# Two pairs of K tiles by seven products in the second half of an output projection too (one core, two-layer hybrid decoder trunk)

## The chip, the cores and the metric

The kernel runs on 1 core of one Trainium2 chip. The metric is the device time of one execution in microseconds (us). Three runs of the kernel before took 2124.72, 2124.95 and 2125.33 us; the median is 2124.95 us. A separate execution was recorded by the hardware profiler; its own time is 2124.64 us, of which the recorded span is 2122.9 us, so 1.74 us lie around the span.

Engine names as the profile has them: PE is the matrix engine, PEld its weight loads, DVE the vector engine, ACT the scalar engine, POOL the GpSimd engine, SP the engine that issues most DMAs (SPq is its queue).

## What is computed

Two layers, each with RMSNorm, a wide input projection, differential attention beside a gated short convolution, one shared output projection and a squared-ReLU MLP. Sequence 256, model width 2048, all in float32. The part that the change touches:

```python
for l in range(DEPTH):                                   # 2 layers
    h = _rmsnorm(x, attn_norm_g[l])
    proj = h @ w_in[l]
    ...
    conv = gate_b * _short_conv(gate_c * conv_in, conv_w[l])
    x = x + jnp.concatenate([attn, conv], axis=-1) @ w_out[l]    # 256x2048 @ 2048x2048
    hm = _rmsnorm(x, mlp_norm_g[l]) @ w_up[l]                    # 256x2048 @ 2048x8192
    x = x + jnp.square(jax.nn.relu(hm)) @ w_down[l]
```

## The kernel before

**Numbers.** A float32 operand is split into a high part (a copy in the type fp32r, made by ACT) and a low part (the operand minus the high part, made by DVE). A product is three matmuls (`TERMS`): high by high, high by low, low by high. A matmul of the output projection has 128 rows of K, 128 tokens as the stationary operand and 512 columns as the moving one.

**Output projection, first 1024 columns.** `BySeven.project` (line 823) computes column chunks 0 and 1 (512 columns each) side by side, in two accumulators of two PSUM banks. K has 16 tiles, taken as eight pairs. A plain pair costs 2 K tiles x 2 token tiles x 2 column chunks x 3 terms = 24 matmuls. Two of the pairs, 4 and 5 (the pairs whose activations are convolution outputs of `GATED`), go by seven products instead of eight (`seven`, line 851): seven products x 3 terms = 21 matmuls, in Winograd's form, with sums of the activations (`sums_of`) and sums of the weights (`BySeven.jobs`, line 777). Four products need accumulators of their own (three `bank` buffers and the `av` bank) until DVE has added them into x: e1 to e4, lines 885 to 901. The order is `self.order`: pairs 0 and 1 for chunk 0, then for chunk 1; seven with pair 4; pair 2; seven with pair 5; pair 3; pairs 6 and 7 for chunk 0 (after which chunk 0 and the e terms are added into x), then pairs 6 and 7 for chunk 1.

**Output projection, last 1024 columns.** The loop at line 984 does chunk 2 and then chunk 3 with `linear` (line 390): 16 K tiles x 2 token tiles x 3 terms = 96 matmuls each, then two additions into x.

**The weights' pipeline.** `Weights.take` hands out the next weight tile and issues the work for the ones up to three ahead (`AHEAD`). A plain job loads 512 KB (`raw`, 4 buffers) and splits it into `hi`/`lo` (`wpool`, 3 buffers). A job of a seven step loads two raws, splits the left one (`w7b`) and a quarter of the right one, and makes four sums (`w7t`) that are split as `w7x` and `w7y`. `w7b` and `w7t` come from `bpool` (8 buffers; four of them hold the projection's activations `cat` and one holds the activation sums `sf`), `w7x` and `w7y` from `apool` (4 buffers, which also hold the transposed parts below).

**From the projection to the MLP.** The MLP's norm is applied in pieces. `Norm.chunk(n)` takes chunk n of x: squares with row sums on ACT, eight transposes on PE into two `bank` buffers, and for each of four K tiles a high part on ACT and a low part on DVE (`split_gained`, line 285), both into tile `nT` n. `Norm.factors` sums the squares, makes the row factors on POOL, a diagonal matrix on DVE and, some ticks later, a matmul with it (`rbc`, line 531), which puts the ratio of the two token tiles' factors on all partitions. The first user of that ratio is the first `square` of the MLP.

**What sets the order.** PE runs in program order. A `Background` list holds pieces of work (generators), and `work.tick()`, called after every K tile of a projection (and after every four matmuls of the MLP's first part), advances them; `work.start(piece, wait)` and the numbers that a piece yields count ticks. DVE, ACT, POOL and SP are ordered by a planner that simulates the program; `late(ins)` keeps an instruction in program order instead. Chunks 0 and 1 are started after the first 1024 columns, with waits of 2 and 4 ticks and 2 more inside, so that their transposes run early in chunk 2's matmuls; chunk 2's run two K tiles into chunk 3's matmuls; chunk 3's run two ticks into the MLP.

**The MLP's start.** `up_part` (line 1147) works on a column of 128 units with half of K at a time: eight matmuls with 512 columns (high and low activations side by side), then eight with 256. The order is column 0 and column 1 with the first half of K (`nT` 0 and 1), then both with the second half (`nT` 2 for four K tiles, then `nT` 3). Every four matmuls tick once.

Of the kernel before, what the change touches and what calls it, by code (L numbers as in the profile page):

```python
# [9 lines left out]
F32 = mybir.dt.float32  # L10
F32R = mybir.dt.float32r
AF = mybir.ActivationFunctionType
ALU = mybir.AluOpType
# [20 lines left out]
NP = DFF // (2 * P)  # L34
LAG = 2
NB2 = DFF // (KG * P)


GATED = (0, 1)

# [82 lines left out]
def trunk(ctx: ExitStack, tc: tile.TileContext, x, w_in, w_out, conv_w, q_norm_g, k_norm_g,  # L123
# [22 lines left out]
    def wide(name):  # L146
        return nat.tile([P, CH], F32, tag="wide", name=name)
# [304 lines left out]
    class Norm:  # L452
# [57 lines left out]
            yield 1  # L510

        def factors(self):
            while self.squared < D // CH:
                yield 1
            tot = small.tile([P, NT], F32, tag="tot", name="tot", bufs=1)
            nc.vector.tensor_reduce(tot, self.ss, axis=AX.X, op=ALU.add)
            r = rstd_of(tot, D, "row", NT)
            self.r = small.tile([P, NT], F32, tag="rowf", name="rowf", bufs=2)
            nc.vector.tensor_copy(self.r, r)
            diag = wide("diag")[:, :NT * P].rearrange("p (t c) -> p t c", t=NT)  # L520
            if self.which:

                self.scale = small.tile([P, 1], F32, tag="rowf2", name="rowf2", bufs=1)
                nc.vector.tensor_mul(self.scale, r[:, 1:2], r[:, 1:2])
                ratio = small.tile([P, 1], F32, tag="ratio", name="ratio", bufs=1)
                nc.vector.reciprocal(ratio, r[:, 1:2])
                nc.vector.tensor_mul(ratio, ratio, r[:, 0:1])
                nc.vector.tensor_scalar_mul(diag[:, 0], ident, ratio)
                yield 8
                tp = bank("rbc")  # L530
                nc.tensor.matmul(tp[:, :P], ones, diag[:, 0], start=True, stop=True)
# [212 lines left out]
    class BySeven:  # L744
# [3 lines left out]
        def __init__(self, l, bpool, weights):  # L748
            self.l, self.pool, self.weights = l, bpool, weights
            n = D // (4 * P)  # L750
            seven = [n + q for q in GATED]
            plain = [i for i in range(2 * n) if i not in seven]


            self.order = [(n, i) for n in range(2) for i in plain[:2]]
            self.order += [step for i, j in zip(plain[2:], seven)
                           for step in (("seven", j), ("pair", i))]
            self.order += [("pair", i) for i in plain[2 + len(seven):-2]]
            self.order += [(n, i) for n in range(2) for i in plain[-2:]]
            self.sums = []  # L760

        def sums_of(self, q, y):
# [11 lines left out]
            nc.scalar.activation(hi, v, AF.Copy)  # L774
            nc.vector.tensor_sub(lo, v, hi.bitcast(F32))

        def jobs(self, w, i):

            mine = {}

            def split(hi, lo, src):
                nc.scalar.activation(hi, src, AF.Copy)
                nc.vector.tensor_sub(lo, src, hi.bitcast(F32))
                return hi, lo

            def two(pool, tag, name, src):

                room = pool.tile([P, 2, 2, CH], F32R, tag=tag, name=name)
                hi, lo = split(room[:, 0], room[:, 1], src)
                return [(hi[:, j], lo[:, j]) for j in range(2)]  # L790

            def plain():
                raws = []
                for n in range(2):
                    raw = self.weights.pool.tile([P, 2, CH], F32, tag="raw", name="raw", bufs=RAW)
                    nc.sync.dma_start(
                        raw, w[2 * P * i:2 * P * (i + 1), n * CH:(n + 1) * CH].rearrange(
                            "(k p) c -> p k c", p=P))
                    raws.append(raw)
                mine["raw"] = raws  # L800
                b11, b21 = two(self.pool, "b", "w7b", raws[0])
                hi = wpool.tile([P, 2, CH], F32R, tag="hi", name="whi")
                lo = wpool.tile([P, 2, CH], F32R, tag="lo", name="wlo")
                return b11, b21, split(hi[:, 0], lo[:, 0], raws[1][:, 1])

            def sums():
                left, right = mine["raw"]
                t = mine["t"] = self.pool.tile([P, 4, CH], F32, tag="b", name="w7t")

                nc.vector.tensor_sub(t[:, 0], right[:, 0], left[:, 0])  # L810
# [12 lines left out]
        def project(self, cat, norm, kpool, tmp):  # L823
            weights = self.weights
            both = [mm.tile([P, NT, CH], F32, tag="mm2", name=f"o{self.l}{n}") for n in range(2)]
# [43 lines left out]

            def onto(n):  # L870
                for t in range(NT):
                    nc.vector.tensor_add(xs[n][:, t], accs[n][t], xs[n][:, t])

            last = self.order[-1][1]
            steps = [i for what, i in self.order if what == "seven"]
            done = [j for j, (what, i) in enumerate(self.order) if what == 0][-1]
            for j, (what, i) in enumerate(self.order):
                if what == "pair":
                    plain(i, 0)
                    plain(i, 1)  # L880
                elif what == "seven":
                    seven(i, i == steps[0], i == steps[-1])
                    if i == steps[-1]:

                        x11, x21, x12, x22 = (xs[n][:, t] for n in range(2) for t in range(NT))


                        room = tmp.tile([P, 2, CH], F32, tag="ao", name="es", bufs=1)
                        e1, e2, e3 = room[:, 0], wide("e2"), room[:, 1]
                        e4 = kpool.tile([P, CH], F32, tag="kL", name="es4")  # L890
                        nc.scalar.activation(e1, prods[1], AF.Copy)
                        nc.vector.tensor_add(e2, prods[6], e1)
                        nc.vector.tensor_add(e4, prods[5], e2)
                        nc.vector.tensor_add(x22, prods[5], x22)
                        nc.vector.tensor_add(e3, prods[7], e2)
                else:
                    plain(i, what)
                    if j == done:
                        onto(0)
                        for x_, e in ((x11, e1), (x12, e4), (x21, e3), (x22, e3)):  # L900
                            nc.vector.tensor_add(x_, x_, e)
            onto(1)
            for n in range(2):
                work.start(norm.chunk(n, 2), 2 * n + 2)


    def mixer(l, norm, loads):

        with ExitStack() as scope:
# [18 lines left out]
            for what, i in by_seven.order:  # L928
                if what == "seven":
                    weights.jobs += by_seven.jobs(w_out[l], i)  # L930
                    continue
                for n in ((0, 1) if what == "pair" else (what,)):
                    weights.plain(w_out[l], 2 * P * i, n * CH, 2)
            for n in range(2, D // CH):
                weights.straight(w_out[l], 0, D // P, n * CH)
            loads(weights)

            bias = biasp.tile([P, 2 * NH, S], F32, tag="bias", name="bias")
# [45 lines left out]
            for n in range(2, D // CH):  # L984
                acc = linear(f"o{l}{n}", cat, weights)
                for t in range(NT):
                    nc.vector.tensor_add(xs[n][:, t], acc[:, t], xs[n][:, t])
                work.start(mnorm.chunk(n, 2))
        return mnorm

    def mlp(l, mnorm, last):
# [479 lines left out]
```

## Time and profile before

| what | us |
|---|---|
| runs, median (lowest to highest) | 2124.95 (2124.72 to 2125.33) |
| profiled execution, its own time | 2124.64 |
| its span | 2122.9 |
| busy: PE, DVE, ACT, POOL | 2117.9, 1724.9, 1376.8, 159.2 |
| layer 0: first 1024 columns of the output projection | 298.17 to 340.36 |
| layer 0: last 1024 columns | 340.36 to 386.71 |
| layer 1: last 1024 columns | 1395.63 to 1441.97 |

The page lists busy times over the span; matmuls are pipelined and a matmul's recorded duration overlaps the next one's, so the time that a matmul costs is read from the start of one stretch to the start of the next in the chain of waits, not from its recorded duration. In the chain of waits each row has a start, a length, the engine, the tile that is written, the line and a count. In a timeline each row has a start, a length, the engine, the line, the operation and what it writes and reads, a count, and in brackets how long the engine stood idle before it and for whom.

### The profile page before, as it was taken

The page shows a single profiled execution, that of the slowest core. Times are in us where ns is not written, and L with a number is a line of the kernel's source. Part 1 is how long each engine was busy: PE and PEld are TensorE (multiplying, and loading weights), DVE is VectorE, ACT ScalarE, POOL GpSimd, SP SyncE. Part 2 cuts the span into 40 slices and gives each one's busy share as a digit, 9 for nine tenths or more (in the row PEclk, how much of TensorE's full clock was granted, in tenths as well). Part 3 has the DMA queues.
Part 4 walks back from the last instruction along what each step waited for, and adds up shares of the span by engine and source line. Part 5 has one row for each costly group of instructions (what it writes and reads, how often), then busy time and mean ns, then how long its engine had stood idle before and what let it go on. Part 6 is the DMA issues. An engine that isn't in the chain of part 4 may idle for free.

```text
span 2122.9 us, 29237 instructions
## 1 busy us (share of the span) xinstructions
PE 2117.9 (100%) x10875; PEld 1812.2 (85%) x10875; DVE 1724.9 (81%) x2388; ACT 1376.8 (65%) x1828; POOL 159.2 (8%) x226
## 2 busy tenths in 40 slices
PE   9999999999999999999999999999999999999999
PEld 8888888888888888888888888888888888888887
DVE  6777677798888888799766776767988888888997
ACT  6777555677776776666566765556677677675664
POOL 3010100000000000011101101000000000000110
PEclk9999999999999999999999999999999999999999
DMA  8556657687777777788656565666877777777993
GB/s 274 177 166 192 195 189 233 213 252 225 231 233 232 235 231 230 253 299 289 217 170 183 164 207 180 199 208 222 259 233 232 232 229 233 233 229 259 319 309 104
DMA packets 297743, 476.01 MB, mean 224 GB/s; under 512 B 12707, under 2 KB 193781, under 8 KB 297600
## 3 DMA queue, kind: packets, MB, share of 16 engines
q1 hardware_dynamic: 269120, 406.76, 60.9%
q0 software_dynamic: 28288, 67.24, 10.0%
q8 instruction: 85, 1.39, 0.3%
q14 instruction: 58, 0.48, 0.1%
q10 hardware_dynamic: 192, 0.15, 0.0%
HBM read 440.52 MB, written 33.58 MB: 223 GB/s over the span
## 4 chain that ended last, share of the span: by engine, by line
PE 100%; DVE 0%; DVEq 0%; issue 0%
PE upc L1158 31%; PE pr L1201 14%; PE dn L1282 8%; PE ci L427 4%; PE gc L427 4%; PE gb L427 4%; PE q L403 4%; PE k L403 4%; PE v L403 4%; PE o L403 4%; PE o L838 3%; PE dn L1364 2%; PE dn L1201 2%; PE pr1r L1201 2%; PE pr0r L1201 1%; PE up L1158 1%
## 5 line engine op out<-in xcount | busy, mean ns | idle before, releaser
L320 DVE TENSOR_TENSOR wlo<-raw,whi 128x1024 fp32r<-128x1024 f32 x266 | 322.3, 1223 | 186.7 <-ACT whi L319 116.6
L1158 PE MATMUL upc<-nT,uhi 128*128 128x512 f32 x1920 | 454.7, 389 | 0.0
L319 ACT ACTIVATE whi<-raw 128x1024 fp32r<-128x1024 f32 x266 | 281.5, 1059 | 240.1 <-issue 29.0
L1158 PEld LDWEIGHTS upc<-nT,uhi 128*128 128x128 f32 x1920 | 360.2, 188 | 74.7
L1022 DVE TENSOR_TENSOR ulo<-uraw,uhi 128x1024 fp32r<-128x1024 f32 x256 | 312.1, 1223 | 118.9 <-ACT f L1190 89.3
L1021 ACT ACTIVATE uhi<-uraw 128x1024 fp32r<-128x1024 f32 x256 | 270.6, 1057 | 159.7 <-PE upc L1158 138.1
L1158 PEld LDWEIGHTS upc<-nT,ulo 128*128 128x128 f32 x1920 | 246.2, 191 | 9.4
L1158 PE MATMUL upc<-nT,ulo 128*128 128x256 f32 x1920 | 249.1, 283 | 0.0
L1282 PE MATMUL dn<-whi,fb 128*128 128x512 f32 x496 | 156.5, 389 | 0.0
L1047 ACT ACTIVATE b2h<-draw 128x1024 fp32r<-128x1024 f32 x83 | 88.1, 1061 | 48.5 <-PE pr L1201 41.3
L319 ACT ACTIVATE whi<-uraw 128x1024 fp32r<-128x1024 f32 x62 | 65.9, 1063 | 81.8 <-PE dn L1282 64.4
L1282 PEld LDWEIGHTS dn<-whi,fb 128*128 128x128 f32 x496 | 93.1, 188 | 19.3
L1168 ACT ACTIVATE ev<-upc 128x512 f32<-128x512 f32 x120 | 72.0, 600 | 53.8 <-PE upc L1158 53.8
L1047 ACT ACTIVATE t24h<-t 128x1024 fp32r<-128x1024 f32 x83 | 88.3, 1063 | 22.9 <-PE pr L1201 15.9
L1048 DVE TENSOR_TENSOR t24l<-t,t24h 128x1024 fp32r<-128x1024 f32 x83 | 101.4, 1221 | 1.7
L1048 DVE TENSOR_TENSOR b2l<-draw,b2h 128x1024 fp32r<-128x1024 f32 x83 | 101.4, 1221 | 1.1 <-ACT b2h L1047 1.1
L1048 DVE TENSOR_TENSOR t13l<-t,t13h 128x1024 fp32r<-128x1024 f32 x83 | 101.3, 1221 | 0.7
L1061 DVE TENSOR_TENSOR t<-draw 128x1024 f32<-128x1024 f32 x83 | 101.4, 1222 | 0.3
L1047 ACT ACTIVATE t13h<-t 128x1024 fp32r<-128x1024 f32 x83 | 88.3, 1064 | 13.3 <-DVE t L1061 2.9
L1282 PE MATMUL dn<-wlo,fb 128*128 128x512 f32 x248 | 96.5, 389 | 0.0
L1201 PE MATMUL pr<-t13h,f 128*128 128x512 f32 x240 | 93.8, 391 | 0.0
L320 DVE TENSOR_TENSOR wlo<-uraw,whi 128x1024 fp32r<-128x1024 f32 x62 | 75.9, 1224 | 17.9 <-ACT whi L319 17.5
(452 smaller groups left out, 4301.4 us busy)
## 6 DMA issues: line engine op xcount, KB each, us to landing
uraw<-in_w_up_dram SPq DMA_DIRECT2D x128, 1024.0 KB, 6.3
raw<-in_w_in_dram SPq DMA_DIRECT2D x191, 512.0 KB, 3.9
draw<-in_w_down_dram SPq DMA_DIRECT2D x174, 512.0 KB, 5.2
raw<-in_w_out_dram SPq DMA_DIRECT2D x64, 512.0 KB, 4.3
uraw<-in_w_down_dram SPq DMA_DIRECT2D x62, 512.0 KB, 5.6
raw<-in_w_down_dram SPq DMA_DIRECT2D x10, 1024.0 KB, 5.7
hid0p<-f POOLq DMA_DIRECT2D x19, 512.0 KB, 3.6
fb<-hid0p POOLq DMA_DIRECT2D x19, 512.0 KB, 7.6
```

What stands on the lines that cost most here:

```text
L319: pair = (nc.scalar.activation(hi, raw, AF.Copy), nc.vector.tensor_sub(lo, raw, hi.bitcast(F32)))
L320: nc.vector.tensor_sub(lo, raw, hi.bitcast(F32)))
L403: nc.tensor.matmul(acc[:, t], a.ap[:, pa, k % KG, t * P:(t + 1) * P], (hi, lo)[pw][:, j], start=(k == 0 and n == 0), stop=(k == nk - 1 and ...
L427: nc.tensor.matmul(acc[:, f, 0] if part else acc[:, f], wt[:, k % 4, fs], a.ap[:, 0, k % KG] if part else a.ap[:, :, k % KG], start=(part ...
L1021: pair = (nc.scalar.activation(hi, src, AF.Copy), nc.vector.tensor_sub(lo, src, hi.bitcast(F32)))
L1022: nc.vector.tensor_sub(lo, src, hi.bitcast(F32)))
L1047: keep(nc.scalar.activation(hi, src, AF.Copy))
L1048: keep(nc.vector.tensor_sub(lo, src, hi.bitcast(F32)))
L1061: keep(nc.vector.tensor_sub(t[:, 0:2], raw[:, :, 1], raw[:, 0]))
L1158: nc.tensor.matmul(acc[:, 0] if part else acc, wt[part][:, k], a.ap[:, 0, k % KG] if part else a.ap[:, :, k % KG], start=(part == 0 and kh ...
L1201: nc.tensor.matmul(prods[n], f[:, pa, a], b[pw], start=(start and m == 0), stop=(stop and m == 2))
L1282: nc.tensor.matmul(prods[p], f[:, pa, 2 * k + t], b[pw][:, n], start=(p in starts and k == 0 and m == 0), stop=(stop and k == 1 and m == 2))
```

## The change

The last 1024 columns of the output projection are done as the first 1024 are: chunks 2 and 3 side by side, and pairs 4 and 5 by seven products. `project` and `jobs` take a `half` or a column, and the loop over `linear` is gone. The second half's order has one more plain pair before the first seven step: pairs 0, 1 for chunk 2, pairs 0, 1 for chunk 3, pair 2, seven (4), pair 3, seven (5), pairs 6, 7 for chunk 2, pairs 6, 7 for chunk 3. In it the quarter of the right weights (`hi`, `lo`) comes from `bpool` as `w7c` instead of `wpool`, and e1 to e4 all come from the `wide` buffers.

The starts of the norm's pieces move: chunk 0's transposes come one tick and chunk 1's three ticks into the second half (before, four and six ticks into chunk 2's matmuls); chunk 2's piece is started where chunk 2 and the e terms have been added into x, and its transposes come four ticks later, which is behind the last matmul of the projection; chunk 3 is as before. The MLP norm's `factors` also waits until the last transposed tile has been issued, its first instruction is kept in program order, and the `rbc` matmul comes 11 ticks behind instead of 8.

```diff
         def factors(self):
-            while self.squared < D // CH:
+            while self.squared < D // CH or (self.which and not self.tiles[-1].ready):
                 yield 1
             tot = small.tile([P, NT], F32, tag="tot", name="tot", bufs=1)
-            nc.vector.tensor_reduce(tot, self.ss, axis=AX.X, op=ALU.add)
+            total = nc.vector.tensor_reduce(tot, self.ss, axis=AX.X, op=ALU.add)
+            if self.which:
+                late(total)
...
-                yield 8
+                yield 11
...
+            self.orders = []
+            for half in range(2):
+                order = [(n, i) for n in range(2) for i in plain[:2]]
+                if half:
+                    order.append(("pair", plain[2]))
+                for i, j in zip(plain[2 + half:], seven):
+                    order += [("seven", j)] + [("pair", i)] * (not half or j != seven[-1])
+                rest = [i for i in plain if not any(i == k for _, k in order)]
+                order += [("pair", i) for i in rest[:-2]]
+                self.orders.append(order + [(n, i) for n in range(2) for i in rest[-2:]])
...
-                hi = wpool.tile([P, 2, CH], F32R, tag="hi", name="whi")
-                lo = wpool.tile([P, 2, CH], F32R, tag="lo", name="wlo")
+                if col:
+                    room = self.pool.tile([P, 2, 2, CH], F32R, tag="b", name="w7c")
+                    hi, lo = room[:, 0], room[:, 1]
+                else:
+                    hi = wpool.tile([P, 2, CH], F32R, tag="hi", name="whi")
+                    lo = wpool.tile([P, 2, CH], F32R, tag="lo", name="wlo")
...
+                        if half:
+                            work.start(norm.chunk(2, 2), 2)
             onto(1)
+            if half:
+                work.start(norm.chunk(3, 2))
+                return
             for n in range(2):
-                work.start(norm.chunk(n, 2), 2 * n + 2)
+                work.start(norm.chunk(n, 1 + n), n)
...
-            by_seven.project(cat, mnorm, kpool, tmp)
-            for n in range(2, D // CH):
-                acc = linear(f"o{l}{n}", cat, weights)
-                for t in range(NT):
-                    nc.vector.tensor_add(xs[n][:, t], acc[:, t], xs[n][:, t])
-                work.start(mnorm.chunk(n, 2))
+            for half in range(2):
+                by_seven.project(cat, mnorm, half, kpool, tmp)
```

More of the change, by code (lines that the diff above doesn't have):

```diff
@@ L796, in plain @@
                     nc.sync.dma_start(
[L797 removed]
+                        raw, w[2 * P * i:2 * P * (i + 1),
+                               col + n * CH:col + (n + 1) * CH].rearrange(
                             "(k p) c -> p k c", p=P))
@@ L821, in jobs, with project @@
             return [plain, sums, more]
-        def project(self, cat, norm, kpool, tmp):
-            weights = self.weights
-            both = [mm.tile([P, NT, CH], F32, tag="mm2", name=f"o{self.l}{n}") for n in range(2)]
+        def project(self, cat, norm, half, kpool, tmp):
+            weights, order = self.weights, self.orders[half]
+            mine = xs[2 * half:2 * half + 2]
+            both = [mm.tile([P, NT, CH], F32, tag="mm2", name=f"o{self.l}{2 * half + n}")
+                    for n in range(2)]
             accs = [[acc[:, t] for t in range(NT)] for acc in both]
@@ L871, in onto @@
                 for t in range(NT):
[L872 to L877, printed above, removed]
+                    nc.vector.tensor_add(mine[n][:, t], accs[n][t], mine[n][:, t])
+            last = order[-1][1]
+            steps = [i for what, i in order if what == "seven"]
+            done = [j for j, (what, i) in enumerate(order) if what == 0][-1]
+            for j, (what, i) in enumerate(order):
                 if what == "pair":
@@ L927, in mixer @@
             by_seven = BySeven(l, bpool, weights)
[L928 to L933, printed above, removed]
-            for n in range(2, D // CH):
-                weights.straight(w_out[l], 0, D // P, n * CH)
+            for half, order in enumerate(by_seven.orders):
+                for what, i in order:
+                    if what == "seven":
+                        weights.jobs += by_seven.jobs(w_out[l], i, 2 * half * CH)
+                        continue
+                    for n in ((0, 1) if what == "pair" else (what,)):
+                        weights.plain(w_out[l], 2 * P * i, (2 * half + n) * CH, 2)
             loads(weights)
```

19 lines of the change are left out of this document (8 added, 11 removed).

## The prediction

> **What bounds the kernel now.** I read the page first (busy times, then the chain of work that ended last), then the chain of waits in order of time around the output projection of both layers, then the timelines of DVE, ACT, POOL and SP from there into the MLP.
>
> ```profile
> span 2122.9 us, 29237 instructions
> ...
> PE 2117.9 (100%) x10875; PEld 1812.2 (85%) x10875; DVE 1724.9 (81%) x2388; ACT 1376.8 (65%) x1828; POOL 159.2 (8%) x226
> ...
> PE 100%; DVE 0%; DVEq 0%; issue 0%
> ```
>
> PE is in use over the whole span and the chain that ended last is all PE: no other engine, and no DMA, ends a wait of any size. So a matmul that goes is worth its place in PE's stream, and anything that becomes late is worth a stall in that stream. In the chain of waits of layer 0, with the first half's seven steps, the second half and the MLP's start:
>
> ```profile
> 309.08 0.68 PE po L863 x3
> 309.76 1.36 PE o L863 x6
> 311.12 2.04 PE po L863 x9
> 313.16 0.68 PE o L863 x3
> 313.84 5.44 PE o L838 x24
> ...
> 340.36 5.44 PE o L403 x24
> 345.80 0.87 PE tpn L473 x8
> ...
> 349.43 0.97 PE tpn L473 x8
> ...
> 367.66 19.06 PE o L403 x84
> 386.71 1.82 PE up L1158 x8
> 388.53 0.87 PE tpn L473 x8
> 389.40 5.59 PE up L1158 x32
> 394.99 0.22 PE rbc L531 x2
> ```
>
> The price of a matmul is read from starts: 24 take 340.36 to 345.80, 5.44 us, so 0.2267 us each. The first seven step runs from 309.08 to 313.84, 4.76 us for 21, again 0.2267 each, and nothing stands between it and its neighbours. The windows view of the second half (PE, PEld, DVE, ACT and POOL busy, each with its count; granted clock; DMA share; GB/s):
>
> ```profile
> 340.36:386.71 46.35, 46.35 (x217) 38.50 (x217) 27.00 (x32) 24.20 (x36) 0.00 (x0) 1.00 0.49 154
> ```
>
> DVE is busy 27.00 of 46.35 us and ACT 24.20, the granted clock is 1.00. There is room beside PE for more DVE work, if it falls at the right places. Layer 1 has the same two starts 46.34 us apart, so what follows counts twice:
>
> ```profile
> 1395.63 5.44 PE o L403 x24
> ...
> 1441.97 1.82 PE up L1158 x8
> ```
>
> **Term 1, the matmuls removed.** The second half is 2 x 96 = 192 matmuls. Afterwards it is six plain pairs of 24 and two seven steps of 21, 186. Six fewer in each layer, twelve in all: 12 x 0.2267 = 2.72 us off. The eight transposes of each chunk (0.87 us) are as many as before, wherever they stand.
>
> [...] The trace has 226.7 ns for this kernel's stream, and the measurement decides.
>
> **Term 2, the sums for the seven steps.** Each step adds DVE and ACT work on the weights. What the two steps of the first half did (DVE, then ACT; the last row is ACT's first split of the second step, behind its raw):
>
> ```profile
> 303.00 0.69 DVE L810 TENSOR_TENSOR w7t<-raw 128x512 f32<-128x512 f32 x1 [1.58 <-DMA raw<-in_w_out_dram]
> ...
> 310.70 1.23 DVE L783 TENSOR_TENSOR w7y<-w7t,w7y 128x1024 fp32r<-128x1024 f32 x1
> ...
> 320.99 1.23 DVE L783 TENSOR_TENSOR w7y<-w7t,w7y 128x1024 fp32r<-128x1024 f32 x1
> ...
> 344.26 1.23 DVE L320 TENSOR_TENSOR wlo<-raw,whi 128x1024 fp32r<-128x1024 f32 x1 [1.44 <-ACT whi L319]
> ...
> 313.37 1.06 ACT L782 ACTIVATE w7b<-raw 128x1024 fp32r<-128x1024 f32 x1 [1.76 <-DMA raw<-in_w_out_dram]
> ```
>
> In the first step the sums begin when the right raw is there (303.00) and the last split, `w7y`, ends at 310.70 + 1.23 = 311.93: 8.93 us. In the second, from 313.37 to 322.22, 8.85 us. PE came to the first use of `w7y` (after 15 of the 21 matmuls, 3.40 us into a step) at 312.48 and 322.68, and did not stop; so margins of 0.5 us are met now. In the second half, call its start T1 (340.36 in layer 0). Seventy-two plain matmuls and two sets of transposes come first, so the first step starts at T1 + 16.32 + 0.87 + 0.97 (the first half's two sets, by their stretches in this trace) = T1 + 18.2 and needs `w7y` at T1 + 21.6. Its right raw takes the room of the fourth tile, whose split ended 345.49 in layer 0, T1 + 5.1; with chunk 0's transposes now ahead of it T1 + 6.0. A raw lands 3.6 us after its issue here:
>
> ```profile
> raw<-in_w_out_dram SPq DMA_DIRECT2D x9, 512.0 KB, 3.6
> ```
>
> That is T1 + 9.6, and 8.93 us later T1 + 18.5: 3.1 us early. The same stretch also carries the low parts of chunks 0 and 1, eight of 0.48 us (rows below), 3.8 us; if all of it came in front, 0.7 us late. The second step starts 4.76 + 5.44 us after the first, T1 + 28.4, and needs `w7y` at T1 + 31.8. Its `w7b` needs a `bpool` room. `cat`, `sf` and the first step's three tiles fill all eight, and PE is done with the first `w7b` six matmuls into that step, at T1 + 19.6 (this wait is new: `w7c` takes the eighth room). 19.6 + 8.85 = T1 + 28.4, 3.4 us early; if the left raw, which needs the first step's sums to be done, is 4 us later, 0.6 us late. What stands behind a waiting split on ACT and DVE is the plain tiles' splits of the next blocks, whose `wpool` rooms are not used by the steps any more, so up to three are ready ahead. Bounds: 0 to 0.7 + 0.6 = 1.3 us for each layer; below nothing is excluded, since PE has no idle time to recover. I take 0, because both margins by these rows are over 3 us.
>
> **Term 3, the way into the MLP.** This is where a stall is most likely. Rows of DVE's timeline: x after the first half, a `nT` part of chunk 0, then the end of the projection.
>
> ```profile
> 334.95 1.29 DVE L872 TENSOR_TENSOR x<-o,x 128x512 f32<-128x512 f32 x2 [0.40 <-PE o L838]
> ...
> 337.89 0.68 DVE L901 TENSOR_TENSOR x<-x,es 128x512 f32<-128x512 f32 x1
> ...
> 349.14 0.88 DVE L288 SCALAR_TENSOR_TENSOR nT<-tpn,gains,nT 128x256 fp32r<-128x256 f32 x2 [0.15 <-ACT nT L287]
> ...
> 386.75 1.29 DVE L987 TENSOR_TENSOR x<-o,x 128x512 f32<-128x512 f32 x2 [0.40 <-PE o L403]
> 387.95 1.22 DVE L1022 TENSOR_TENSOR ulo<-uraw,uhi 128x1024 fp32r<-128x1024 f32 x1
> 389.09 0.15 DVE L516 TENSOR_REDUCE tot<-ss 128x2 f32<-128x8 f32 x1
> ...
> 391.60 0.16 DVE L519 COPY rowf<-row_r 128x2 f32<-128x2 f32 x1
> ...
> 391.73 0.48 DVE L288 SCALAR_TENSOR_TENSOR nT<-tpn,gains,nT 128x256 fp32r<-128x256 f32 x1
> ...
> 393.16 0.28 DVE L528 TENSOR_SCALAR diag<-ident,ratio 128x128 f32<-128x128 f32 x1
> 393.35 0.48 DVE L288 SCALAR_TENSOR_TENSOR nT<-tpn,gains,nT 128x256 fp32r<-128x256 f32 x1
> ```
>
> The groups of the stretch from 296 to 402 us, and POOL's part of the row factors:
>
> ```profile
> L288 DVE SCALAR_TENSOR_TENSOR nT<-tpn,gains,nT 128x256 fp32r<-128x256 f32 x16 | 7.1, 479 | 0.5 <-ACT nT L287 0.3
> L287 ACT ACTIVATE nT<-tpn,gains 128x256 fp32r<-128x256 f32 x16 | 6.8, 467 | 4.4 <-DVE nT L288 4.4
> ...
> L491 ACT ACTIVATE junk<-x 128x512 f32<-128x512 f32 x8 | 4.9, 618 | 0.9 <-DVE x L901 0.9
> ```
>
> ```profile
> 389.60 0.70 POOL L449 TENSOR_TENSOR row_r<-row_e,mhalf 128x2 f32<-128x2 f32 x1
> ```
>
> Before: PE ends the projection at 386.71 and needs the last K tile of `nT` 3 when? The 32 up matmuls from 389.40 end with the eight of 512 columns that use `nT` 2 and 3; these eight are 1.82 us long (the row at 386.71), so they start at 394.99 - 1.82 = 393.17, use `nT` 3 from 394.08, and its last K tile at 394.76. DVE's last low part ends 393.35 + 0.48 = 393.83. So 0.9 us are left, and PE does not stop.
>
> After, with T0 the projection's last matmul: chunk 2's additions must be done first. In the first half the same six additions began 334.95 when PE finished chunk 0's part and ended 338.57, 3.6 us later, with one weight split between them; 24 matmuls (5.44 us) follow in the second half too, so x is ready 1.8 us before T0 and chunk 2's transposes take T0 to T0 + 0.87. Everything of PE behind them is 0.87 us later: `nT` 2 is needed at T0 + 7.33, `nT` 3 from T0 + 8.24, its last K tile at T0 + 8.92. Chunk 0's low parts ended 350.02, 3.35 us behind its transposes (345.80 + 0.87); so chunk 2's end near T0 + 4.2, 3.1 us early. Chunk 3's transposes end at T0 + 0.87 + 1.82 + 0.87 = T0 + 3.56, and at the old distance (393.83 - 389.40 = 4.43) its parts end at T0 + 8.0, again 0.9 us early. What is new in that stretch: four low parts (4 x 0.479 = 1.9 us of DVE) and four high ones (4 x 0.467 = 1.9 us of ACT) of chunk 2. What leaves it: the six small instructions of `factors` between 389.09 and 393.44, of 0.15 to 0.28 us, about 1.0 us, which now stand behind the parts. DVE: x, two `ulo` of 1.22, `factors` and four low parts, 6.7 us in 7.1 before; 7.6 in 8.9 after. It fits, with little left, and the two engines hand over to each other (ACT's next pair waits for DVE's last). Bounds: 0, and, if the whole of chunk 2's 3.35 us is served ahead of chunk 3's, 8.0 + 3.35 - 8.92 = 2.4 us a layer. Queued behind a late low part on DVE is only the next `ulo`.
>
> `rbc` comes three ticks later. At T0 + 8.28 + 0.87 + 0.98 + 0.91 = T0 + 11.0 (its old distance, 394.99 - 386.71; the new transposes; eight matmuls of 256 columns, (5.59 - 2 x 1.82) / 2; four of 512) PE stops if the diagonal isn't there. `factors` now starts at T0 + 8.0 to 8.9; from the sum to POOL's result took 389.09 to 390.30, 1.2 us, and from `rowf` to `diag` 391.60 to 393.44, 1.8 us with low parts between, 1.0 us without. So it is there at T0 + 10.2 to 11.9: 0 to 0.9 us of stall, less if PE was already held. For both together I take 0.3 us a layer, near the low end, since the sums of both engines' work fit.
>
> **The other edits** cost nothing that shows: chunks 0 and 1's earlier transposes find x ready (338.57, before 340.36) and free banks; e1 to e4 in `wide` buffers only move. The raw loads are the same 512 KB in number; the DMA share of 0.49 in the second half covers them, and without that cover each late raw holds one 2.72 us block. The MLP's first weight loads sit behind them on SP as before.
>
> **The sum.** Against the profiled execution: 2124.64 - 2.72 + 2 x 0 + 2 x 0.3 = 2122.5 us. The median of the runs is 0.31 us above that execution, so I say 2122.8 us, 0.10% faster.
>
> **The rivals.**
>
> *Chunk 2 ahead of chunk 3 (slower).* With both chunks' parts in one stretch, ACT and DVE serve chunk 2 and the weight splits first, and the first `up` columns wait for `nT` 3. Against it: the 1.3 us of DVE that the sum above leaves. For it: a margin of only 0.9 us now. Price 2.4 us a layer: 2124.95 - 2.72 + 4.8 = 2127.0. It decides from 1.36 us a layer.
>
> *The sums come late.* The rooms of `bpool` or the raws hold the second seven step; 1.3 us a layer gives 2124.95 - 2.72 + 2.6 = 2124.8, no gain. For it: the first half's margin of 0.5 us; against it: over 3 us by the rows. Both rivals together give 2129.6, slower by 0.22%.
>
> *It doesn't do what it says.* The removed matmuls would be worth less than their place, down to the weight load alone, 38.50 us for 217 in the second half, 0.177 us each: 2124.95 - 12 x 0.177 + 0.6 = 2123.4. Against it: 21 and 24 matmuls have the same price to 0.1%. [...]
>
> *More than the matmuls.* A gain of over 4.3 us needs a stall of now that goes; the chain shows none. 2120.
>
> **Chances.** Forecast (stalls of 0 to 0.8 us a layer, 2122.2 to 2123.8) 0.65; chunk 2 ahead of chunk 3 0.14; late sums 0.08; both 0.07; less than its place 0.03; more 0.03. The range 2121.9 to 2127.2 leaves out both together, the gain beyond the matmuls and some of the first rival's upper end. Within 0.2% (4.25 us, about what a measurement of this kernel can tell from no change) lie 2120.7 to 2129.2: faster 0.03, slower 0.10 (both, and a first rival with a longer wait), same 0.87.
>
> **What would show it.** Right: seven steps of 4.76 us at L863 four times a layer, second halves of 42.2 us plus transposes, no PE wait before `up` or `rbc`. Wrong: idle PE before `up` with DVE or ACT `nT` as releaser (first rival, term 3), before L863 with `w7b` or `w7y` (second, term 2), or starts of 24 matmuls that are no longer 5.44 us apart.

## The result, and the profile after

| kernel | median of the runs, us | lowest to highest | ratio to before, 95% interval |
|---|---|---|---|
| before | 2125.06 | 2124.72 to 2125.37 | 1 |
| after | 2130.86 | 2128.48 to 2132.06 | 1.0026 [1.0016, 1.0036] |

The change makes the kernel 5.8 us, 0.26%, slower. The profiled execution took 2132.06 us, 1.76 us more than its span; it is the slowest of the ten runs, so its trace shows the upper end of the loss. The page of the changed kernel, its span and its busy times:

```profile
span 2130.3 us, 29269 instructions
...
PE 2120.3 (100%) x10863; PEld 1813.0 (85%) x10863; DVE 1750.9 (82%) x2428; ACT 1383.0 (65%) x1838; POOL 159.3 (7%) x226
```

Twelve matmuls are gone (10863 for 10875), and the span is 7.4 us longer. What PE waited for, after the change, in all, times and longest:

```profile
PE tpn L472 <- DVE nT L287: 3.9, 2, 1.9
```

Before the change PE had no wait but at the very start (1.1 us). Now there are 1.9 us in each layer before a set of transposes (`tpn`), behind the low parts (`nT`) of DVE; in the two halves PE also waits 1.0 us for `wlo` and 0.2 us for `w7y`, in both layers together. The chain of waits in layer 0 (line 854 is the plain block, 879 the seven step, 1177 the `up` part):

```profile
324.63 16.33 PE o L854 x72
...
364.94 5.44 PE o L854 x24
370.38 0.68 PE po L879 x3
...
375.14 10.90 PE o L854 x48
...
391.73 9.04 PE up L1177 x44
...
402.86 7.18 PE upw L1177 x39
```

The matmuls cost what they did: 24 in 364.94 to 370.38, 5.44 us; a seven step in 370.38 to 375.14, 4.76 us. The second half runs from 324.63 + 16.33 = 340.96 to 375.14 + 10.90 = 386.04, 45.08 us. 186 matmuls and two sets of transposes are 42.16 + 1.84 = 44.00, so 1.08 us are lost inside it. From there to `upw` it is 402.86 - 386.04 = 16.82 us; before it was 398.96 - 386.71 = 12.25, and with chunk 2's transposes, now there, 13.12. So 3.70 us are lost behind the projection. Layer 1, the same view:

```profile
1383.22 16.33 PE o L854 x72
...
1433.94 10.90 PE o L854 x48
...
1461.63 8.54 PE upw L1177 x45
```

Second half 1399.55 to 1444.84, 45.29 us, 1.29 lost; then 16.79 us, 3.67 lost. Together 1.08 + 1.29 + 3.70 + 3.67 = 9.7 us lost against 2.72 saved. Most of it lies in the ten microseconds behind the projection; PE there, in layer 0:

```profile
385.86 1.03 PE L472 MATMUL tpn<-ident,x 128*128 128x128 f32 x8
386.65 2.08 PE L1177 MATMUL up<-nT,uhi 128*128 128x512 f32 x8
388.57 0.60 PE L472 MATMUL tpn<-ident,x 128*128 128x128 f32 x4
391.10 0.63 PE L472 MATMUL tpn<-ident,x 128*128 128x128 f32 x4 [1.93 <-DVE nT L287]
...
392.52 3.56 PE L1177 MATMUL up<-nT,uhi 128*128 128x512 f32 x8
```

Chunk 2's transposes (eight), eight `up` matmuls, half of chunk 3's transposes; then PE stands still for 1.93 us before the other half. Behind the stop the row of eight `up` matmuls is 3.56 us long (392.52); eight of the same form ahead of it took 2.08 (386.65). The windows view, one microsecond a row (busy PE, PEld, DVE, ACT, POOL with counts, then the granted clock, DMA share and GB/s), shows the clock there:

```profile
392.00:393.00 1.00, 1.00 (x8) 0.91 (x7) 1.00 (x3) 0.44 (x2) 0.00 (x0) 0.79 1.10 345
393.00:394.00 1.00, 1.00 (x4) 0.81 (x3) 1.00 (x2) 0.27 (x1) 0.00 (x0) 0.50 0.99 299
394.00:395.00 1.00, 1.00 (x3) 0.74 (x3) 0.41 (x2) 0.00 (x0) 0.42 (x2) 0.50 1.03 369
395.00:396.00 1.00, 1.00 (x4) 0.77 (x3) 0.46 (x4) 0.00 (x0) 0.47 (x1) 0.51 0.99 401
396.00:397.00 1.00, 1.00 (x10) 1.00 (x9) 0.28 (x1) 0.82 (x1) 0.00 (x0) 1.00 1.05 418
```

The granted clock falls to 0.50 after the stop and is back at 1.00 at 396. By the rows it is low for 0.42 + 1 + 1 + 0.98 = 3.40 us (0.79 over one microsecond is 0.42 us at 0.50). So the loss behind the projection seems to have two parts: a stop of 1.93 us, and 3.70 - 1.93 = 1.77 us for matmuls at half the clock, where 3.40 us at half the clock would make 1.70, an estimate from these rows.

What does PE wait for? The next block is not a view of the profile but the order of instructions in the program that the changed kernel builds, with notes behind the rows: the first two rows are PE's, the rest DVE's, and the last number of a name counts the tile:

```
L472 tpn3_0_3826<-ident_97,x3_87          [waits DVE]
L472 tpn3_1_3835<-ident_97,x3_87          [waits DVE, PE]
...
L287 nT10_2_3712<-tpn2_0_3717             first of chunk 2
L287 nT10_2_3712<-tpn2_1_3726             second
L287 nT10_2_3712<-tpn2_0_3717             third: now bank tpn2_0 has been read
L287 nT10_3_3821<-tpn3_0_3826
```

Four sets of transposes (`tpn2_0`, `tpn2_1`, `tpn3_0`, `tpn3_1`) follow each other with eight matmuls between, and there are three `bank` buffers, handed out in turn. A set fills one of them with two K tiles. The fourth set needs the first one's bank (the program gives `tpn2_0` and `tpn3_1` the same one), which is free when ACT and DVE have made the parts of both of its K tiles. On ACT that part of the stretch is:

```profile
387.44 0.62 ACT L490 ACTIVATE junk<-x 128x512 f32<-128x512 f32 x1
...
389.02 1.05 ACT L1040 ACTIVATE uhi<-uraw 128x1024 fp32r<-128x1024 f32 x1
389.97 1.19 ACT L286 ACTIVATE nT<-tpn,gains 128x256 fp32r<-128x256 f32 x3
```

The squares (`junk`) and a weight split stand between the parts, so that the third high part begins at 389.97, 4.1 us behind the start of chunk 2's transposes (385.86). DVE follows:

```profile
390.46 1.27 DVE L287 SCALAR_TENSOR_TENSOR nT<-tpn,gains,nT 128x256 fp32r<-128x256 f32 x3 [1.20 <-ACT nT L286]
```

The third low part of chunk 2 ends near 390.46 + 0.48 = 390.94, and PE goes on at 391.10. Until here this is a reading of the trace; the runs below test it.

### The profile page after: what moved, and what is told of

Read it like the earlier page. It is cut to its first block, busy times and chain, and to the rows that moved or that the text cites. A ratio compares the mean times of both kernels' runs of the same rounds, so it can differ in the third digit from the quotient of the medians.

```text
span 2130.3 us, 29269 instructions
## 1 busy us (share of the span) xinstructions
PE 2120.3 (100%) x10863; PEld 1813.0 (85%) x10863; DVE 1750.9 (82%) x2428; ACT 1383.0 (65%) x1838; POOL 159.3 (7%) x226
## 4 chain that ended last, share of the span: by engine, by line
PE 98%; DMA 1%; DVE 1%; ACT 1%; issue 0%; DVEq 0%; ACTq 0%
PE upc L1177 31%; PE pr L1220 14%; PE dn L1301 8%; PE o L854 5%; PE ci L426 4%; PE gc L426 4%; PE gb L426 4%; PE k L402 4%; PE v L402 4%; PE q L402 4%; PE dn L1383 2%; PE dn L1220 2%; PE pr1r L1220 2%; PE pr0r L1220 1%; PE upw L1177 1%; PE up L1177 1%
## 5 line engine op out<-in xcount | busy, mean ns | idle before, releaser
L319 DVE TENSOR_TENSOR wlo<-raw,whi 128x1024 fp32r<-128x1024 f32 x258 | 312.3, 1223 | 161.7 <-ACT whi L318 91.6
L318 ACT ACTIVATE whi<-raw 128x1024 fp32r<-128x1024 f32 x258 | 273.0, 1059 | 232.3 <-issue 35.4
L854 PE MATMUL o<-whi,cat 128*128 128x512 f32 x384 | 121.1, 390 | 0.0
```

Source lines behind the costliest of these rows:

```text
L318: pair = (nc.scalar.activation(hi, raw, AF.Copy), nc.vector.tensor_sub(lo, raw, hi.bitcast(F32)))
L319: nc.vector.tensor_sub(lo, raw, hi.bitcast(F32)))
L854: nc.tensor.matmul(accs[n][t], a.ap[:, pa, k % KG, t * P:(t + 1) * P], (hi, lo)[pw][:, j], start=(k == 0 and m == 0), stop=(i == last and ...
```

## The experiments

All ratios are to the kernel before, run beside each kernel on the same chip.

### A fourth bank, no seven steps, matmuls in the gap, old factors

**e1**, one more bank for the fourth set, the `av` bank, which is free there:

```diff
-                tp = bank(f"tpn{n}_{j}")
+                if self.which and (n, j) == (3, 1):
+                    tp = ps.tile([P, CH], F32, tag="av", name=f"tpn{n}_{j}", bufs=1)
+                else:
+                    tp = bank(f"tpn{n}_{j}")
```

> The changed kernel with one edit: the last of the four sets of transposes behind the projection (chunk 3, second) writes into the av bank instead of a fourth use of the three bank buffers. Theory (bank): PE's stop before that set, 1.9 us in each layer, is a wait for the first of chunk 2's two banks, and the slow matmuls behind it (eight up matmuls in 3.36 us instead of 1.82) are a consequence of the stop. Then the stop and the lower clock go in both layers: 2 x 3.7 us less, about 2123.5 us. Rival (parts): the parts themselves are late, so PE stops later, before nT 3 is used; then the time stays within 2 us of 2130.9. Rival (sums): the loss lies in the second half's seven steps; then under 1 us changes.

2123.85 us (2123.45 to 2124.81), ratio 0.9995 [0.9986, 1.0004]: 7.0 us less than the changed kernel. The chain of waits of this run, layer 0:

```profile
385.32 0.88 PE tpn L475 x8
386.20 1.83 PE up L1180 x8
...
398.46 11.13 PE upw L1180 x64
```

From 385.32 to 398.46 are 13.14 us, the 13.12 that the work needs, and layer 1 has 13.14 too; there is no stop before the fourth set, and the eight `up` matmuls of 512 columns behind it are a row of 2.00 us (389.69), at a granted clock of 1.00. The parts were never too late for `up`. What was late was a bank. The run is 1.1 us faster than before the change; its own runs and those of before do not overlap much (before: 2124.66 to 2125.59), but the interval reaches past 1.

**e2**, the second half side by side, but all pairs plain (`orders[1]` with every "seven" as "pair", and no e terms).

> The changed kernel with its second half side by side, but pairs 4 and 5 as plain pairs (192 matmuls, no sums). Theory (bank): the stop behind the projection is the order's, not the sums': it stays, 3.7 us a layer, while the 1.1 and 1.3 us lost inside the two halves go and the saving of 2.7 us goes with them: about 2125.1 + 7.4 = 2132.5 us. Rival (sums): with the sums gone the loss goes too: about 2125 us.

2130.66 us (2129.09 to 2132.45), ratio 1.0028 [1.0016, 1.0040]. The profile has the same stop before `tpn`, 1.93 us in each layer, and a clock of 0.998; its own execution took 2132.17 us. No wait is left inside the two halves. The median is 1.8 us under the expected number: executions of this form scatter over 3 us, as those of the changed kernel do. So the seven steps have no part in the stop.

**e3**, eight matmuls of 512 columns between chunk 3's two sets of transposes.

```diff
+                if self.which and (n, j) == (3, 1):
+                    filler[0]()
                 tp = bank(f"tpn{n}_{j}")
...
+                    def fill(acc=two[1], a=mT[0]):
+                        for _ in range(8):
+                            nc.tensor.matmul(acc, a.ap[:, 0, 0, :P], a.ap[:, :, 0],
+                                             start=True, stop=True, skip_group_check=True)
```

> The changed kernel with eight extra matmuls of 512 columns (1.8 us, into an accumulator that the MLP overwrites afterwards) between the two sets of chunk 3's transposes, where PE stops. They add nothing to the result. Theory (bank, with the clock): the stop itself cannot shrink, but the matmuls behind it keep the full granted clock, so 1.5 us a layer come back: about 2128 us, granted clock 1.00. Rival (no clock effect): the matmuls behind the stop are slow for another reason (operands late, DMA traffic): 2131 us or more, and the eight up matmuls still take over 3 us.

2128.72 us (2128.15 to 2129.80), ratio 1.0018 [1.0009, 1.0027]: 2.1 us less than the changed kernel, with more work. PE in layer 0, and the windows row of the stretch in which the clock fell after the change:

```profile
389.04 2.10 PE L1237 MATMUL up<-nT 128*128 128x512 f32 x8
391.22 0.63 PE L475 MATMUL tpn<-ident,x 128*128 128x128 f32 x4
...
392.64 2.00 PE L1180 MATMUL up<-nT,uhi 128*128 128x512 f32 x8
```

```profile
390.00:395.00 5.00, 4.92 (x30) 4.05 (x30) 3.79 (x8) 2.87 (x8) 0.30 (x2) 1.00 1.00 339
```

The stretch without matmuls is filled, the second set still comes at 391.2, but the eight `up` matmuls behind it are a row of 2.00 us, where the changed kernel has 3.56, and the granted clock is 1.00. It is 1.000 in all ten runs of e3, for 0.998 in seven of the changed kernel's ten: with eight matmuls in the place of the stop the clock did not fall. From the projection's end to `upw` this run takes 15.27 us in each layer, 2.15 over the work, where the changed kernel lost 3.70 and 3.67. Between these two profiled executions that is 1.55 + 1.52 = 3.07 us, which I put down to the clock; the medians are 2.1 us apart.

**e4**, the row factors as before the change (no wait for the last tile, nothing in program order, 8 ticks).

> The changed kernel with the MLP norm's row factors as before (not held behind the last transposed tile, first instruction free, rbc 8 ticks behind). Theory (bank): the factors are not the cause; the small instructions then stand among the parts again and take about 1 us of DVE there, so PE stops 0 to 1 us longer in each layer: 2131 to 2133 us. Rival (factors): holding them back is what costs: under 2128 us.

2129.72 us (2127.92 to 2131.58), ratio 1.0022 [1.0012, 1.0031]. Neither expected number; the stop is there (3.9 us in the two layers, 1.96 in layer 0), and with executions that scatter over 3.7 us this run does not tell the two apart. The edit is measured again below, where no bank is waited for.

### The same stop without the rest of the change, and without a fourth bank

**e6**, the kernel before with chunk 2's piece put off, nothing else:

```diff
-                work.start(mnorm.chunk(n, 2))
+                work.start(mnorm.chunk(n, 16 if n == 2 else 2))
```

> The kernel before with one edit: chunk 2's piece of the norm waits 16 ticks, so that its transposes come behind the projection's last matmul, as in the changed kernel. No seven steps in the second half. Theory (bank): four sets of transposes within ten matmuls against three banks make the same stop and the same slow matmuls: 3.7 us a layer, 2132 us, granted clock under 1.00. Rival (the stop needs the sums or the new starts): 2125 to 2127 us.

2130.70 us (2128.92 to 2132.61), ratio 1.0024 [1.0015, 1.0034]. One start moved makes the unchanged kernel as slow as the changed one. PE, layer 0:

```profile
391.44 0.63 PE L473 MATMUL tpn<-ident,x 128*128 128x128 f32 x4 [1.96 <-DVE ratio L526]
...
393.19 3.24 PE L1158 MATMUL up<-nT,uhi 128*128 128x512 f32 x8
```

The trace names `ratio` as releaser, since the row factors of this kernel still stand among DVE's parts. The same gap, and the same slow eight matmuls (3.24 us for the 2.00 of e3).

**e7**, the changed kernel with three banks and another order in the second half:

```diff
-                self.orders.append(order + [(n, i) for n in range(2) for i in rest[-2:]])
+                order += [(n, i) for n in range(2) for i in rest[-2:]]
+                if half:
+                    order = order[:6] + [(0, 3), (0, 6), ("seven", 5), (0, 7), (1, 3), (1, 6), (1, 7)]
+                self.orders.append(order)
```

> The changed kernel (three banks, no av) with another order in the second half: pairs 3 and 6 of chunk 2 stand between the two seven steps, then pair 7 of chunk 2, then pairs 3, 6, 7 of chunk 3; chunk 2 is complete 36 matmuls before the end instead of 24, and its transposes come 12 matmuls before the projection's last. Theory (bank): its banks are free before chunk 3's second set, the stop goes: 2123.5 to 2125 us. Rival (any late chunk 2 costs): over 2128 us.

2123.81 us (2123.33 to 2124.63), ratio 0.9995 [0.9986, 1.0004], clock 1.000, no wait before `tpn`. Twelve matmuls (2.7 us) between chunk 2's transposes and the projection's end do what a fourth bank does.

### What is lost inside the second half

With the stop gone (e1), twelve matmuls less would be 2125.06 - 2.72 = 2122.3 us; 1.5 us are still missing. In the changed kernel PE's weight loads wait inside the two halves for two things (in all, times, longest), and the chain of waits of layer 0 shows what the larger wait hangs on:

```profile
PEld o L854 <- DVE wlo L319: 1.9, 2, 0.9
...
PEld po L879 <- DVE w7y L792: 0.9, 2, 0.6
```

```profile
343.44 5.79 DMA raw<-in_w_out_dram
...
349.25 1.07 ACT w7b L791
...
351.97 0.60 DVE w7t L824
...
353.17 1.15 DVE wlo L319
...
354.36 5.60 PE o L854 x23
```

The raw behind the first seven step's `w7b` lands 5.79 us after its issue, where the forecast had 3.6. That 3.6 was the median of a stretch of the kernel before that has no seven steps (345 to 400 us); in the stretch with the first half's steps (296 to 345 us) the median was 4.7. On DVE the low part of pair 2 (`wlo`), which PE needs next, stands behind that raw's `w7b` and two sums, and comes when PE has already stopped. The smaller wait, for `w7y`, is the same kind of thing one block on. ACT in layer 0 of e1, and the chain there:

```profile
357.39 1.06 ACT L318 ACTIVATE whi<-raw 128x1024 fp32r<-128x1024 f32 x1 [3.89 <-DMA raw<-in_w_out_dram]
359.30 1.06 ACT L318 ACTIVATE whi<-raw 128x1024 fp32r<-128x1024 f32 x1 [0.85 <-DMA raw<-in_w_out_dram]
360.26 1.04 ACT L794 ACTIVATE w7y<-w7t 128x1024 fp32r<-128x1024 f32 x1
```

```profile
361.54 1.23 DVE w7y L795
```

The two splits of pair 3 (line 318) stand ahead of `w7y` on ACT and wait 3.89 and 0.85 us for their raws; on DVE their low parts stand ahead of `w7y` too. It is there at 361.54 + 1.23 = 362.8, a little after PE needs it.

**e9**, pair 3's splits kept in program order, so behind `w7y` (an argument `keep` through `plain` and `halves` to `late`):

```diff
-                        weights.plain(w_out[l], 2 * P * i, (2 * half + n) * CH, 2)
+                        weights.plain(w_out[l], 2 * P * i, (2 * half + n) * CH, 2,
+                                      keep=bool(half) and i == 3)
```

> The kernel with the av bank with the two splits of each pair 3 of the second half kept in program order, so that they stand behind w7y instead of ahead of it. Theory (queue): PE's waits for w7y in both layers go, some 1.5 us together: 2122.3 to 2122.9 us. Rival (crowding, or late raws as such): w7y comes as late as before, 2123.5 us or more; or pair 3 is late in its place, over 2124 us.

2130.27 us (2129.63 to 2133.76), ratio 1.0028 [1.0017, 1.0038]: far from the theory's number. It lies in the range of the rival, but pair 3 is not late in its place, and the `w7y` that is late is another one. The waits of PE in this run, and its chain, show that the wait moved one step on:

```profile
PE po L882 <- DVE w7y L795: 1.9, 2, 1.0
PE po L882 <- ACT w7y L794: 1.7, 2, 1.1
```

```profile
367.98 4.29 DMA raw<-in_w_out_dram
...
372.37 1.07 ACT whi L318
...
374.69 1.15 DVE w7y L795
```

Now pair 6's split stands ahead of the second step's `w7y` and waits for its raw, and PE stops there, 1.7 us for the high part and 1.9 us for the low one in the two layers. The mean granted clock of this execution is 0.999.

**e10**, the same with pairs 3 and 6 (`i in (3, 6)`).

> The kernel with the av bank with the splits of pairs 3 and 6 of the second half in program order, so that they stand behind w7y of both seven steps on ACT and DVE. Theory (queue): in the run with pair 3 alone in program order the wait only moved to the second step, where pair 6's splits stood ahead of w7y; with both behind, PE stops for neither: 2122.3 to 2123.2 us. Rival (late raws): the second step's raws come too late in any order: over 2126 us.

2123.38 us (2122.89 to 2124.16, 11 runs), ratio 0.9992 [0.9984, 1.0001], 0.2 us above the theory's range. The kernel before beside it had 2124.48 to 2125.48, so the two sets of runs lie apart, though the interval just reaches past 1. No wait for `w7y` is left. The chain, and the only wait on PE's weight loads in the two halves:

```profile
324.71 16.34 PE o L857 x72
...
374.55 10.88 PE o L857 x48
...
398.57 6.50 PE upw L1181 x36
```

```profile
PEld o L857 <- DVE wlo L319: 1.1, 2, 0.6
```

The second half takes 341.05 to 385.43, 44.38 us, 0.38 over the work in it; the end 13.14. This is the fastest version that was run, 1.6 us or 0.08% under before. The wait that is left is for pair 2's low part (`wlo`), on DVE behind the first step's `w7b` and sums; no run takes it away.

**e11**, e7's order with chunk 2's pairs 3, 6 and 7 in program order.

> The order with chunk 2 complete 36 matmuls before the end, three banks, with chunk 2's plain pairs 3, 6 and 7 in program order behind w7y. Theory (queue): PE's waits for w7y (0.9 us on PE, 1.7 us on its weight loads, both layers) go: 2122.3 to 2123.2 us. Rival (late raws): 2124 us or more.

2124.24 us (2123.00 to 2125.07), ratio 0.9995 [0.9986, 1.0004]: the rival's number. PE waits for no `w7y` any more (e7: 0.9 us), but 1.0 us for a plain pair's `wlo` (e7: 0.3) and, new, 0.8 us for x, ahead of chunk 2's transposes: no gain over e7.

**e8**, e1 with chunks 0 and 1 started as before the change.

> The kernel with the av bank (2123.85 us) with chunks 0 and 1 of the norm started as before the change (four and six ticks into the second half instead of one and three). What is left there over the sum of 2122.3 us is lost inside the two second halves. Theory (queue): a plain pair's splits stand on ACT and DVE ahead of w7y and wait for their raws; the starts do not matter much: 2123.3 to 2125 us. Rival (crowding): the early parts of chunks 0 and 1 are in the way; without them under 2123.0 us.

2133.99 us (2133.72 to 2134.76), ratio 1.0044 [1.0031, 1.0056], 10 us more than e1 and far from both numbers. PE stops at the other place where four sets of transposes stand close together, inside chunk 1's two sets, and ACT shows why:

```profile
353.90 1.09 PE L475 MATMUL tpn<-ident,x 128*128 128x128 f32 x4 [3.83 <-DVE nT L287]
```

```profile
348.31 1.06 ACT L794 ACTIVATE w7b<-raw 128x1024 fp32r<-128x1024 f32 x1 [0.43 <-DMA raw<-in_w_out_dram]
350.26 0.63 ACT L794 ACTIVATE w7c<-raw 128x512 fp32r<-128x512 f32 x1 [0.89 <-DMA raw<-in_w_out_dram]
```

Chunk 0's parts now stand behind `w7b` and `w7c`, which wait for the raws of the first seven step, and chunk 1's second set waits 3.83 us for chunk 0's bank. The earlier starts of the change keep this stop away.

**e12**, e1 with the row factors as before the change.

> The kernel with the av bank with the row factors as before the change. It isolates that edit where no bank is waited for. Theory: the small instructions stand among the parts again, and a last part of nT 3 comes up to 1 us later with 0.9 us to spare: 2123.5 to 2125 us. Rival (holding the factors back costs something, at rbc): under 2123.3 us.

2124.23 us (2123.74 to 2125.53), ratio 0.9997 [0.9988, 1.0006], as the theory had it: 0.4 us more than e1, within the scatter of both. Holding the factors back gains at most that.

## Why the forecast failed

**What failed: term 3, the way into the MLP.** Its words were that chunk 3's parts end "again 0.9 us early", and "for both together I take 0.3 us a layer". It asked when `up` needs the parts, and that part was right: in e1 and e10 the stretch takes 13.14 us, with nothing lost. The step that failed is that it never asked where the transposes write. Chunk 2's two sets and chunk 3's two need four banks within eight matmuls, and there are three; the only place where the prediction spoke of banks was for chunks 0 and 1 ("free banks"). What stood on the path was not the last part but the third one of chunk 2, which frees the bank. The price was 3.70 and 3.67 us a layer, over the upper bound of 2.4. The bound was the serial parts alone, with no clock in it. Without the fall of the clock the loss is 2.15 us a layer (e3), which is inside the bound, though by another mechanism; the clock's share is 3.07 of the 7.37 us.

**Term 1 was right.** 12 x 0.2267 = 2.72 us: matmuls cost the same after the change, 5.44 us for 24 and 4.76 for 21. From the start of layer 0's projection to the end of the span the kernel before takes 2122.9 - 298.17 = 1824.73 us and e10 2121.5 - 298.85 = 1822.65, 2.08 us less. That is 2.72 less the 0.38 and 0.43 us that e10 loses in its two halves, and 0.1 us a layer more, by which the kernel before was over the work in its second half (46.35 and 46.34 us for 46.24). The median shows 1.6.

**Term 2 was mis-sized.** I took 0 of 0 to 1.3 us a layer; it was 1.08 and 1.29, at the upper bound. The step that failed is the sentence that behind a waiting split stand "the plain tiles' splits of the next blocks", of which "up to three are ready ahead". In the trace the split behind the waiting `w7b` is that of the pair PE is at (`wlo`, 1.9 us of waits in the two layers), and a plain pair's split that waits for a raw itself stands ahead of `w7y` (0.9 us). For `w7y` that is shown: e9 moves the wait, e10 takes it away. For `wlo` it is read from the chain, and no run tested it; in e10 it is 1.1 us. The landing time of 3.6 us, read from a stretch without seven steps, was too short as well: the raw in the chain took 5.79.

**The rivals.** "Chunk 2 ahead of chunk 3" named the right stretch, with DVE's `nT` as releaser, and the right sign; its mechanism (nT 3 late for `up`) was wrong, and its price, 2.4 us a layer, 2127.0, too small. "The sums come late" is a small part of the truth. "Both" at 2129.6 is the nearest number, and it had 0.07; as a bank and the clock made the larger part of the loss, that it came near is chance.

**The smaller steps.** x was ready when expected: no set of transposes waits for it. `rbc` never stopped PE. That moving chunks 0 and 1's starts costs nothing is not shown by itself: one of their low parts (0.48 us of DVE) stands in the chain ahead of the late `wlo`. Why they had to move was not seen: without it e8 loses ten microseconds.

**The sum as it should have been:** 2124.64 - 2.72 + 1.08 + 1.29 + 3.70 + 3.67 = 2131.7 us against 2132.06 of the profiled execution. The other 0.4 us do not come from the part that was changed: layer 0's projection begins 0.59 us later in the execution profiled after the change (298.76 for 298.17), most of it in the 22 `warm` matmuls at the program's start (5.06 us for 4.54), and the 0.1 us a layer named above go off. e6, which is the kernel before up to there, is 0.53 us late there as well (340.89 for 340.36).

## What to carry to other kernels

When work of two groups is moved together, count the buffers that all of it holds at once, PSUM banks first, and follow who frees the first of them; that the results come in time for their user is a second question. On an engine without idle time a stop need not be worth its length alone: here 1.93 us of stop came with 1.55 and 1.52 us of slower matmuls behind it, so read the granted clock there too. And an instruction that waits for a transfer can cost what stands behind it on its engine: in e9 pair 6's split waited 1.33 us for its raw ahead of `w7y`, and PE stood still for 1.09 us. Forcing one such instruction back only handed the wait to the next.

## What the runs showed that was not expected

The granted clock fell to 0.50 after a stop that was short, 1.93 us in the trace. In layer 0 of the changed kernel it was low for 3.40 us; in layer 1 the rows are

```profile
1450.00:1451.00 1.00, 1.00 (x9) 1.00 (x10) 0.85 (x3) 0.82 (x2) 0.00 (x0) 0.85 1.02 348
...
1454.00:1455.00 1.00, 1.00 (x7) 0.88 (x6) 0.18 (x3) 0.03 (x1) 0.70 (x2) 0.94 0.98 385
```

with three rows of 0.50 between: 0.30 + 3 + 0.12 = 3.42 us. In layer 0 of e8, with its stop of 3.83 us (350.07 to 353.90), it was low for longer:

```profile
352.00:353.00 1.00, 0.00 (x0) 0.00 (x0) 1.00 (x2) 1.00 (x3) 0.00 (x0) 0.62 0.08 29
...
358.00:359.00 1.00, 1.00 (x3) 0.77 (x3) 0.80 (x3) 0.95 (x1) 0.00 (x0) 0.50 0.82 309
```

All rows between are at 0.50 as well: 0.76 + 6 = 6.76 us up to 359.

A fall does not begin at a fixed distance from the stop either. In the changed kernel the two begin at 392.58 and 1450.70, 1.48 and 0.80 us behind the stop's end; in e8 the one of layer 0 begins at 352.24, while PE stands still. No run shows what sets the beginning or the length.

Nor does the same stop always bring a fall. In e4 the two stops are 3.9 us together, 1.96 in layer 0; the 32 `up` matmuls behind them take 6.97 us in layer 0 and 5.59, as before the change, in layer 1, and the mean granted clock is 0.999 for the 0.998 of the changed kernel. In e9 PE stops for 1.09 and 0.95 us in layer 0, and the 48 matmuls behind take 10.88 us, as in e10.

One fall of 3.4 us at 0.50 is 0.0008 of the span in the mean clock, and by that costs half its length, 1.7 us, an estimate; e3 gave 1.55 and 1.52. The scatter of the runs agrees: of the changed kernel's ten, the fastest (2128.48 us) has a mean granted clock of 1.000, the next two (2129.47 and 2129.66) have 0.999, and the seven from 2130.79 to 2132.06 have 0.998. The runs of e2 fall into the same three steps (2129.09; 2130.37 to 2130.75; 2132.17 and 2132.45 us), and so do those of e6 (2128.92 to 2129.25; 2130.55 to 2130.84; 2132.61).
